# Two encoder layers: x stored by halves, a reordered beginning, and the second half's leading products between the layers taken from x without its token factors

## The chip, the cores and the metric

The kernel runs on one core of one Trainium2 chip. The metric is the device time of one execution in microseconds (us). The kernel before took 1564.54 us, the median of three runs (1564.0 to 1566.41). Its trace comes from one profiled execution. In the trace and in this text the engines are: PE or TensorE (products; PEld is its loading of weights), DVE or VectorE, ACT or ScalarE, POOL or GpSimd, and SP, whose queue issues most of the loads. ACTq and POOLq are the queues on which ScalarE and GpSimd issue loads.

## The reference

Two layers (DEPTH 2) of an encoder work on a residual stream x of 512 tokens by 1024 channels in float32. Cut to what matters:

```
mem_n = rms_norm(mem, mem_norm_g)
for l in range(DEPTH):
    h = rms_norm(x, g_pre_mix[l])
    proj = h @ w_in[l]
    q_a, k_a, v_a, q_b, k_b, v_b, q_m, gate_pre = split(proj)
    o_a = neighborhood_attention(q_a, k_a, v_a)      # 6 heads
    o_b = dilated_attention(q_b, k_b, v_b)           # 6 heads in 3 groups
    o_m = memory_attention(q_m, mem_n, w_mem_kv[l])  # 4 heads, 256 memory tokens
    merged = sum of sigmoid(gate_pre + b_gate) * (o @ w_br) over the three branches
    x = x + rms_norm(merged @ w_out[l], g_post_mix[l])
    h = rms_norm(x, g_pre_ffn[l])
    a, b = split(conv3(h @ w_up[l]))
    x = x + rms_norm((gelu(a) * b) @ w_down[l], g_post_ffn[l])
```

`rms_norm(x, g)` is `x * rsqrt(mean(x*x) + 1e-6) * g`, with the mean over the 1024 channels of a token. A token's factor, the reciprocal root, is one number per token; the gain g is one number per channel.

## The kernel before, in words

**Layout.** x is held transposed: channels on the 128 partitions in 8 chunks (KD = 8), 512 tokens along the free dimension. The tokens are worked in two halves of 256 (HALVES) wherever a norm has to be waited for. x lives in two tiles of four chunks by 512 tokens each; load_x fetches two chunks of one half in each of four DMAs (L190-L192).

**Products.** Each weight tile of 128 output channels is loaded raw in float32 on SP's queue (L225), and split into a high part by ScalarE and a low part (raw minus high) by VectorE or GpSimd (split, L218; weights, L222). Activations are split in the same way, and mm3 (L244) makes one product of three: high by high, high by low, low by high. In the trace all products of mm have line L242; transposes have L253; VectorE's and ScalarE's operations go through a counting wrapper and all have L114, so they are told apart by their tiles: whi and wlo (or m, h) from wraw are the split weights; h from x, vec, pt is a normed chunk; y, x, acc and sq belong to the ends of sublayers; ka are key tiles; pt, s, o and mm are banks of PSUM. There are three mm banks, two s banks, two pt banks and one o bank.

**Order of the work.** The class Woven writes TensorE's order by hand. It keeps a clock `clk` that adds a planned cost for each product, and a heap of jobs (Python generators) with due times: a job yields a delay or a flag to wait for, and is stepped when the clock has come to its due time, at the ticks between the products. So a job's small TensorE steps are placed among the large products by planned times (`yield 0.8`, `yield lat`). TensorE runs in that order; the order on the other engines is set by the framework's scheduler, which goes by the order of issue and by its own model of when an instruction is ready, and the buffers of one tag are handed out in turn.

**Small steps.** rstd_job (L321) makes the tokens' factors: products with a column of 1/1024 sum the squares over the partitions, ScalarE takes the root, VectorE the reciprocal, and a product with the identity spreads the factors over all partitions (L338). pre_norm_job (L359) then makes h by normed (L340): one VectorE operation with gain and factor, then a split. end_job (L373) ends a sublayer: it multiplies the sublayer's output by its factors, adds it to x, sums the squares of x and, if given, goes on with the next pre-norm. factor_end_job (L388) does the same but splits x times the gain without the token factors (raw_split); the factors R are multiplied in after the product. It serves the up-projection (after the mixing sublayer), not the boundary between the layers.

**The leading group.** The six projections that a layer begins with (FIRST: queries, keys and values of the first two head pairs) run as a group in pairs: run_group (L466) takes a pair of tiles through all eight chunks for one half of the tokens. Their banks come from group_banks (L463): two mm, two s, o and pt. The layer loop (L850) runs the group for the first half, then for the second; both wait for h of their half. Then a_q, a_k and a_v split the results, a_v also rearranges the values, and v_job transposes them. The first heads wait for the transposed values.

**The beginning.** The first half of x is loaded, squared and summed (first_squares, L825); then the first two weights are loaded and split, the second half of x is loaded, and the other four weights follow. vec, with all gains and biases, is loaded on GpSimd's queue near the top (L205).

**Between the layers.** In the down-projection of layer 0 (sublayer_end, L779) the last output tile is done by halves. At its beginning mem_norm_job is spawned for layer 1: it loads and norms the memory tokens, its squares by ScalarE and their sum by GpSimd (L316). The memory's key and value products of layer 1 (mem_kv) come after the last down-projection tile; mem_v_job transposes their values into an s bank. Then layer 1's leading group begins.

Of the kernel before, what the change touches and what calls it, by code (L numbers as in the profile page):

```python
# [14 lines left out]
SEQ = 512  # L15
# [12 lines left out]
FIRST = (0, 3, 6, 1, 4, 7)  # L28
# [91 lines left out]
def tile_hybrid_encoder(ctx, tc, xT, memT, memg, vecs, rpb, w_in, w_kv, w_bra, w_brb, w_brm,  # L120
# [84 lines left out]
    nc.gpsimd.dma_start(out=vec, in_=vecs)  # L205
# [115 lines left out]
    def rstd_job(accs, n, box):  # L321
# [37 lines left out]
    def pre_norm_job(l, goff, acc, hs, i):  # L359
        half, box = HALVES[i], []  # L360
        yield from rstd_job(acc if isinstance(acc, list) else [acc[:, half]], 256, box)
        for k in range(KD):
            normed(x[k][:, half], vec[:, l, goff + k:goff + k + 1], box[0], hs[k][0][:, half], hs[k][1][:, half],
                   G if k in LOG[l > 0 and goff == V_PRE] else V)
# [8 lines left out]
    def end_job(l, goff, og, acc, acc2, i, then, lat, more=()):  # L373
# [3 lines left out]
        for k in range(KD):  # L377
            V.tensor_mul(og[k][:, half], og[k][:, half], box[0])
            (G if then is None and i and k in TAILG else V).tensor_add(x[k][:, half], x[k][:, half], og[k][:, half])
            if acc2 is not None:  # L380
                sumsq_add(acc2[:, half], x[k][:, half], k == 0, None, G if k in SQG[goff == V_POSTF] else V)
            else:
                nc.sync.dma_start(out=out[:, k, half], in_=x[k][:, half])
# [4 lines left out]
    def factor_end_job(l, goff, og, acc, acc2, i, nxt):  # L388
# [5 lines left out]
        for k in range(KD):  # L394
            V.tensor_mul(og[k][:, half], og[k][:, half], box[0])
            V.tensor_add(x[k][:, half], x[k][:, half], og[k][:, half])
            raw_split(l, gnext, k, x[k][:, half], h[k][0][:, half], h[k][1][:, half])
# [4 lines left out]
        for k in range(KD):  # L402
            sumsq_add(acc2[:, half], x[k][:, half], k == 0)
# [4 lines left out]
        if i == 1:  # L408
            yield 0.6
            wv.give(f"R{l}.{gnext}")  # L410

# [51 lines left out]
    def group_banks():  # L463
        return [mmbank(), mmbank(), sbank(), sbank(), obank(128), tbank()]

    def run_group(grp, hs, half, flag, cols=None, side=2):  # L466
        if flag and side == 2:
# [3 lines left out]
        for i in range(0, len(ws), side):  # L471
            for k in range(n):
                if flag and side > 2:
                    wv.need(f"{flag}.{k}")
                rhs = [t[:, half] for t in hs[k]]
# [66 lines left out]
    def a_v(ps, qkv, flag):  # L542
# [5 lines left out]
        V.tensor_copy(vv[:, 0, :, 8:16], ps3[:, :, 0:8])  # L548
        V.tensor_copy(vv[:, 0, :, 0:8], ps3[:, :, 56:64])
# [229 lines left out]
    def sublayer_end(l, goff, w_of, rhs, n_half, then, lat=(1.4, 1.8), mid=None, fill=()):  # L779
# [26 lines left out]
        for i, half in enumerate(HALVES):  # L806
# [12 lines left out]
            if isinstance(then, tuple):  # L819
# [5 lines left out]
    def first_squares(half):  # L825
        sqs = [ytile((128, 256)) for _ in range(KD)]
        for k in range(KD):
            ACT.activation(sqs[k], x[k][:, half], AF.Square)
            if k % 2:
                V.tensor_add(sqs[k], sqs[k], sqs[k - 1])  # L830
            if k in (3, 5):
# [235 lines left out]
```

## Time and profile before

| | us |
|---|---|
| median of 3 runs | 1564.54 |
| profiled execution | 1565.1 |
| its span (first to last instruction) | 1563.3 |
| PE busy | 1524.4 |
| DVE busy | 945.2 |
| ACT busy | 735.1 |
| POOL busy | 155.2 |

A row of a timeline reads: start, time, engine, line, operation, out<-in, shape, how many were merged, and in brackets how long the engine had been idle and who ended that. Products are pipelined, so the time of a single one is longer than the distance to the next start; distances between starts are what the stream costs. A row of windows gives, for a stretch of time, each engine's busy time with its instructions, then the granted clock of TensorE (1.00 is full) and the DMA engines' share.

### The profile page before, as it was taken

The numbers are of one execution on the slowest core, as the hardware profiler recorded it, in microseconds if no ns is written. First come the engines' busy times: TensorE is split into PE (matmuls) and PEld (weight loads), VectorE is DVE, ScalarE is ACT, GpSimd is POOL, SyncE is SP. The second block draws the span as 40 slices with busy tenths as digits, with TensorE's granted clock in tenths as the row PEclk, the third lists the DMA queues.
The fourth block names the chain that finished last, engine by engine and source line by source line (L and its number), as shares of the span: only waits on it lengthen the run. The fifth ranks groups of instructions, "written<-read, shape, count | busy, mean of one in ns | idle before, by whom it ended". The sixth has DMA issues, their size and how long they took to land.

```text
span 1563.3 us, 20698 instructions
## 1 busy us (share of the span) xinstructions
PE 1524.4 (98%) x7994; PEld 1303.7 (83%) x7994; DVE 945.2 (60%) x1682; ACT 735.1 (47%) x1267; POOL 155.2 (10%) x219
## 2 busy tenths in 40 slices
PE   6999999999999999999989999999999999999997
PEld 6888888888988888788889888888889888888887
DVE  6685566235777777742385856753456877775233
ACT  5564575236544444522344645743364544444231
POOL 4340000210000000100061400001100000000000
PEclk9999999999999999999989999999999999999999
DMA  7222113325113322333331221132250222333331
GB/s 244 88 79 72 61 57 96 93 95 163 54 56 101 100 94 95 104 98 101 115 115 44 80 69 63 56 108 81 95 189 15 81 95 95 94 100 96 98 103 63
DMA packets 46610, 144.90 MB, mean 93 GB/s; under 512 B 5232, under 2 KB 11376, under 8 KB 46512
## 3 DMA queue, kind: packets, MB, share of 16 engines
q1 hardware_dynamic: 44656, 139.61, 28.2%
q10 hardware_dynamic: 1152, 2.10, 0.5%
q0 software_dynamic: 704, 1.88, 0.4%
q8 instruction: 62, 1.02, 0.3%
q14 instruction: 36, 0.29, 0.1%
HBM read 141.47 MB, written 2.10 MB: 92 GB/s over the span
## 4 chain that ended last, share of the span: by engine, by line
PE 54%; DVE 3%; issue 0%; ACT 0%; ACTq 0%; DVEq 0%
PE mm L242 48%; PE s L242 3%; PE o L242 2%; PE pt L242 1%; PE pt L253 1%; DVE y L114 1%; DVE x L114 1%; DVE m L114 0%; DVE acc L114 0%; DVE wlo L114 0%; DVE ka L114 0%; DVE st L114 0%; ACT sq L114 0%; ACT y L114 0%; ACT m L114 0%
## 5 line engine op out<-in xcount | busy, mean ns | idle before, releaser
L242 PE MATMUL mm<-h,whi 128*128 128x512 f32 x2496 | 775.7, 392 | 0.0
L242 PEld LDWEIGHTS mm<-h,whi 128*128 128x128 f32 x2496 | 461.5, 188 | 90.9
L242 PE MATMUL mm<-h,wlo 128*128 128x512 f32 x1248 | 486.4, 390 | 0.0
L114 DVE TENSOR_TENSOR wlo<-wraw,whi 128x1024 fp32r<-128x1024 f32 (+1 forms) x213 | 259.8, 1221 | 293.9 <-ACT whi L114 291.5
L114 ACT CAST whi<-wraw 128x1024 fp32r<-128x1024 f32 (+1 forms) x213 | 221.0, 1039 | 318.5 <-PE mm L242 310.4
L242 PEld LDWEIGHTS mm<-h,wlo 128*128 128x128 f32 x1248 | 234.3, 188 | 49.9
L242 PE MATMUL mm<-m,whi 128*128 128x512 f32 (+1 forms) x800 | 216.3, 358 | 2.7 <-ACT whi L114 1.8
L242 PEld LDWEIGHTS mm<-m,whi 128*128 128x128 f32 x800 | 142.5, 190 | 25.1 <-ACT whi L114 2.2
L242 PE MATMUL mm<-m,wlo 128*128 128x512 f32 (+1 forms) x400 | 142.8, 357 | 1.2 <-DVE wlo L114 1.2
L114 DVE SCALAR_TENSOR_TENSOR y<-y,vec,y 128x511 f32<-128x511 f32 x176 | 130.9, 750 | 3.5 <-ACT y L114 0.9
L114 DVE TENSOR_TENSOR y<-mm,R 128x512 f32<-128x512 f32 x82 | 56.4, 688 | 68.5 <-PE mm L242 68.5
L242 PEld LDWEIGHTS mm<-m,wlo 128*128 128x128 f32 x400 | 75.9, 190 | 12.5 <-DVE wlo L114 1.6
L766 POOL TENSOR_TENSOR m<-m,y 128x512 f32<-128x512 f32 x28 | 36.1, 1288 | 405.7 <-DVE y L114 405.7
L114 ACT ACTIVATE y<-y,vec 128x512 f32<-128x512 f32 x88 | 71.0, 813 | 2.2 <-DVE y L114 1.9
L242 PE MATMUL mm<-m,m 128*128 128x512 f32 x240 | 63.6, 395 | 0.0
L114 ACT ACTIVATE y<-y 128x512 f32<-128x512 f32 x44 | 27.8, 632 | 72.0 <-DVE y L114 71.5
L242 PE MATMUL s<-h,m 128*128 128x256 f32 x384 | 54.7, 290 | 5.4 <-DVE m L114 5.4
L114 ACT ACTIVATE y<-mm,vec 128x512 f32<-128x512 f32 (+1 forms) x91 | 57.4, 631 | 0.1
L242 PE MATMUL mm<-h,m 128*128 128x256 f32 x360 | 54.6, 298 | 2.8 <-DVE h L114 1.8
L114 ACT CAST m<-pt 128x512 fp32r<-128x512 f32 (+1 forms) x72 | 38.2, 539 | 40.4 <-PE pt L253 32.0
L114 DVE TENSOR_TENSOR acc<-acc,sq 128x256 f32<-128x256 f32 (+1 forms) x80 | 40.5, 507 | 26.2 <-ACT sq L114 24.6
L114 DVE TENSOR_TENSOR m<-pt,m 128x512 fp32r<-128x512 f32 (+1 forms) x72 | 45.0, 629 | 18.3 <-ACT m L114 17.4
(143 smaller groups left out, 1762.5 us busy)
## 6 DMA issues: line engine op xcount, KB each, us to landing
wraw<-in_w_in_dram SPq DMA_DIRECT2D x88, 512.0 KB, 3.4
wraw<-in_w_up_dram SPq DMA_DIRECT2D x88, 512.0 KB, 3.3
wraw<-in_w_down_dram SPq DMA_DIRECT2D x32, 512.0 KB, 3.5
wraw<-in_w_out_dram SPq DMA_DIRECT2D x16, 512.0 KB, 4.2
wraw<-in_w_down_dram SPq DMA_DIRECT2D x16, 384.0 KB, 3.1
wraw<-in_w_kv_dram SPq DMA_DIRECT2D x8, 512.0 KB, 4.4
wraw<-in_w_bra_dram SPq DMA_DIRECT2D x16, 192.0 KB, 2.3
x<-in_xT_dram SPq DMA_DIRECT2D x8, 256.0 KB, 6.9
```

The costliest lines, as they stand in the source:

```text
L114: return op(*args, **kw)
L242: wv.pe(nc.tensor.matmul(ps, a, b, start=first, stop=last), cost)
L253: wv.pe(nc.tensor.transpose(ps[:, 128 * i:128 * i + 128], s, ident), 0.11)
L766: (V if br == 2 and m >= 6 else G).tensor_add(acc[m], acc[m], gs)
```

## The change

- x is one tile of two halves, each of 8 chunks by 256 tokens, and the host lays xT out in the same way, so that a load of two chunks of a half is one run of 2 KB per partition. `xh(k, half)` replaces `x[k][:, half]` everywhere.
- The gains of layer 0's first norm come in a small tile g0 (128 by 8), loaded first on ScalarE's queue. vec moves from GpSimd's queue to SP's, behind the loads of the second half of x.
- first_squares adds the first half's squares only in pairs, and the sum over four tiles is left to the products.
- The low part of the second weight moves from GpSimd to VectorE. Two idle products of zeros into the o bank are put first in TensorE's order.
- The spread in rstd_job becomes a transpose.
- FIRST and group_banks change their order alike: each tile keeps its kind of bank, but the pair in o and pt comes second and the pair in the s banks last.
- Between the layers the second half goes through the new raw_end_job. Its leading products are taken from x times the gain, without token factors, as soon as each chunk is there; afterwards each of the six banks is multiplied by R for that half. h of the second half is also made, for the later projections.
- mem_norm_job of layer 1 is spawned with a delay of 20.
- The two edge copies in a_v move from VectorE to ScalarE.

```diff
-FIRST = (0, 3, 6, 1, 4, 7)
+FIRST = (0, 3, 4, 7, 6, 1)
...
-    xs = [const.tile([128, 4, 512], F32, name=f"x{i}") for i in range(2)]
-    x = [xs[k // 4][:, k % 4, :] for k in range(KD)]
+    xs = const.tile([128, 2, KD, 256], F32, name="x")
+
+    def xh(k, half):
+        return xs[:, half.start // 256, k, :]
...
-            nc.sync.dma_start(out=xs[k // 4][:, k % 4:k % 4 + 2, half], in_=xT[:, k:k + 2, half])
-
+            i = half.start // 256
+            nc.sync.dma_start(out=xs[:, i, k:k + 2, :], in_=xT[:, i, k:k + 2, :])
+
+    g0 = const.tile([128, KD], F32, name="g0")
+    nc.scalar.dma_start(out=g0, in_=vecs[:, 0, V_PRE:V_PRE + KD])
     load_x(HALVES[0])
...
-    nc.gpsimd.dma_start(out=vec, in_=vecs)
...
-            mm(pr[:, 128 * b:128 * b + 128], spread, ident, True, True, 0.22)
+            wv.pe(nc.tensor.transpose(pr[:, 128 * b:128 * b + 128], spread, ident), 0.11)
...
+    def raw_end_job(l, goff, og, acc, acc2, nxt, lat):
+
+
+        half, box = HALVES[1], []
+        hs, raw, R = nxt
+        yield lat
+        raw.extend((t[:, 0, :], t[:, 1, :]) for t in [ktile(F32R, (128, 2, 256)) for _ in range(KD)])
+        yield from rstd_job([acc[:, half]], 256, box)
+        for k in range(KD):
+            V.tensor_mul(og[k][:, half], og[k][:, half], box[0])
+            V.tensor_add(xh(k, half), xh(k, half), og[k][:, half])
+            raw_split(l + 1, V_PRE, k, xh(k, half), *raw[k])
+            if k == 0:
+                yield 0.6
+            wv.give(f"raw{k}")
+            yield 1.05
+        for k in range(KD):
+            sumsq_add(acc2[:, half], xh(k, half), k == 0)
+        yield 3.5
+        box = []
+        yield from rstd_job([acc2[:, half]], 256, box)
+        ACT.copy(R[:, half], box[0])
+        wv.give("R")
+        for k in range(KD):
+            normed(xh(k, half), vec[:, l + 1, V_PRE + k:V_PRE + k + 1], box[0], hs[k][0][:, half], hs[k][1][:, half])
+        crit[0] = last_copy[0]
+        yield 1.2
+        wv.give(f"h{l + 1}.{V_PRE}.1")
...
-        return [mmbank(), mmbank(), sbank(), sbank(), obank(128), tbank()]
+        return [mmbank(), mmbank(), obank(128), tbank(), sbank(), sbank()]
...
-        V.tensor_copy(vv[:, 0, :, 8:16], ps3[:, :, 0:8])
-        V.tensor_copy(vv[:, 0, :, 0:8], ps3[:, :, 56:64])
+        ACT.copy(vv[:, 0, :, 8:16], ps3[:, :, 0:8])
+        ACT.copy(vv[:, 0, :, 0:8], ps3[:, :, 56:64])
...
-            if k in (3, 5):
+            if k in (3, 5) and half != HALVES[0]:
                 V.tensor_add(sqs[k], sqs[k], sqs[k - 2])
-        return sqs[5::2]
-
+        return sqs[1::2] if half == HALVES[0] else sqs[5::2]
+
+    idle_bank = obank(128)
+
+    def idle(n):
+
+        one, none = mean[:, 0:1], zero[:, 0:1]
+        a, b = (bass.AP(t.tensor, t.offset, [list(t.ap[0]), [0, w]]) for t, w in ((one, 128), (none, 512)))
+        for _ in range(n):
+            mm(idle_bank, a, b, True, True, 0.0)
+
+    idle(2)
     hs = h_tiles()
     wv.spawn(pre_norm_job(0, V_PRE, first_squares(HALVES[0]), hs, 0))
-    gw = group_weights([w_in[0, m] for m in FIRST[:2]], (V, G))
+    gw = group_weights([w_in[0, m] for m in FIRST[:2]], (V, V))
     load_x(HALVES[1])
+    nc.sync.dma_start(out=vec, in_=vecs)
...
-        for i in range(2):
-            run_group((gw, pss), hs, HALVES[i], f"h{l}.{V_PRE}.{i}")
+        run_group((gw, pss), hs, HALVES[0], f"h{l}.{V_PRE}.0")
+        if l == 0:
+            run_group((gw, pss), hs, HALVES[1], f"h{l}.{V_PRE}.1")
+        else:
+            run_group((gw, pss), raw, FULL, "raw", HALVES[1], 2, True)
+            wv.need("R")
+            for ps in pss:
+                V.tensor_mul(ps[:, HALVES[1]], ps[:, HALVES[1]], R[:, HALVES[1]])
+            wv.need(f"h{l}.{V_PRE}.1")
...
-            wv.spawn(mem_norm_job(l + 1, hm, htile))
-            box, pre = [], []
+            wv.spawn(mem_norm_job(l + 1, hm, htile), 20.0)
+            pre, R, raw, box = [], rtile(), [], []
...
-            sublayer_end(l, V_POSTF, w_of, fs, 1, then, (1.4, LAT1), lambda: wv.spawn(kv_ahead()))
+            sublayer_end(l, V_POSTF, w_of, fs, 1, [then, (box, raw, R)], (1.4, LAT1), lambda: wv.spawn(kv_ahead()))
```

More of the change, by code (lines that the diff above doesn't have):

```diff
@@ L362, in pre_norm_job @@
         for k in range(KD):
-            normed(x[k][:, half], vec[:, l, goff + k:goff + k + 1], box[0], hs[k][0][:, half], hs[k][1][:, half],
+            g = g0[:, k:k + 1] if l == 0 and goff == V_PRE else vec[:, l, goff + k:goff + k + 1]
+            normed(xh(k, half), g, box[0], hs[k][0][:, half], hs[k][1][:, half],
                    G if k in LOG[l > 0 and goff == V_PRE] else V)
@@ L378, in end_job @@
             V.tensor_mul(og[k][:, half], og[k][:, half], box[0])
-            (G if then is None and i and k in TAILG else V).tensor_add(x[k][:, half], x[k][:, half], og[k][:, half])
+            (G if then is None and i and k in TAILG else V).tensor_add(xh(k, half), xh(k, half), og[k][:, half])
             if acc2 is not None:
-                sumsq_add(acc2[:, half], x[k][:, half], k == 0, None, G if k in SQG[goff == V_POSTF] else V)
+                sumsq_add(acc2[:, half], xh(k, half), k == 0, None, G if k in SQG[goff == V_POSTF] else V)
             else:
-                nc.sync.dma_start(out=out[:, k, half], in_=x[k][:, half])
+                nc.sync.dma_start(out=out[:, k, half], in_=xh(k, half))
         if then is not None:
@@ L395, in factor_end_job @@
             V.tensor_mul(og[k][:, half], og[k][:, half], box[0])
-            V.tensor_add(x[k][:, half], x[k][:, half], og[k][:, half])
-            raw_split(l, gnext, k, x[k][:, half], h[k][0][:, half], h[k][1][:, half])
+            V.tensor_add(xh(k, half), xh(k, half), og[k][:, half])
+            raw_split(l, gnext, k, xh(k, half), h[k][0][:, half], h[k][1][:, half])
             if k == 0:
@@ L410, in factor_end_job @@
             wv.give(f"R{l}.{gnext}")
+    def raw_end_job(l, goff, og, acc, acc2, nxt, lat):
[6 more added lines that the diff above has]
+            V.tensor_mul(og[k][:, half], og[k][:, half], box[0])
+            V.tensor_add(xh(k, half), xh(k, half), og[k][:, half])
+            raw_split(l + 1, V_PRE, k, xh(k, half), *raw[k])
[4 more added lines that the diff above has]
+        for k in range(KD):
+            sumsq_add(acc2[:, half], xh(k, half), k == 0)
+        yield 3.5
[8 more added lines that the diff above has]
+        wv.give(f"h{l + 1}.{V_PRE}.1")
     def h_tiles():
@@ L463, in group_banks, with run_group @@
     def group_banks():
-        return [mmbank(), mmbank(), sbank(), sbank(), obank(128), tbank()]
-    def run_group(grp, hs, half, flag, cols=None, side=2):
-        if flag and side == 2:
+        return [mmbank(), mmbank(), obank(128), tbank(), sbank(), sbank()]
+    def run_group(grp, hs, half, flag, cols=None, side=2, each=False):
+        each = each or side > 2
+        if flag and not each:
             wv.need(flag)
@@ L472, in run_group @@
             for k in range(n):
-                if flag and side > 2:
-                    wv.need(f"{flag}.{k}")
-                rhs = [t[:, half] for t in hs[k]]
+                if flag and each:
+                    wv.need(f"{flag}{k}")
+                rhs = [t[:, half] if half != FULL else t for t in hs[k]]
                 for w, ps in zip(ws[i:i + side], pss[i:i + side]):
@@ L818, in sublayer_end @@
                         post_norm_tile(l, goff, m, ps, og, acc, half, n0 == 0 and len(order) + len(pair) == KD and m == pair[0])
-            if isinstance(then, tuple):
+            if isinstance(then, list) and i:
+                wv.spawn(raw_end_job(l, goff, og, acc, acc2, then[1], lat[1]))
+            elif isinstance(then, list):
+                wv.spawn(end_job(l, goff, og, acc, acc2, 0, lambda i: then[0](acc2, i), lat[0]))
+            elif isinstance(then, tuple):
                 wv.spawn(factor_end_job(l, goff, og, acc, acc2, i, then))
@@ L900, in tile_hybrid_encoder @@
         for i in range(2):
-            run_group((gw, list(pss.values())), hs, HALVES[i], f"h{l}.{V_PREF}.{i}", None, 4)
+            run_group((gw, list(pss.values())), hs, HALVES[i], f"h{l}.{V_PREF}.{i}.", None, 4)
         fs, held, flag = [], [], f"R{l}.{V_PREF}"
```

10 lines of the change are left out of this document (4 added, 6 removed).

## The prediction

> **What bounds the kernel now.** I read the page first, then TensorE's timeline over the whole span for every wait it shows, then the timelines of the other engines around the three longest waits.
>
> ```profile
> span 1563.3 us, 20698 instructions
> PE 1524.4 (98%) x7994; PEld 1303.7 (83%) x7994; DVE 945.2 (60%) x1682; ACT 735.1 (47%) x1267; POOL 155.2 (10%) x219
> ```
>
> The profiled execution took 1565.1 us, 1.8 us more than its span; the median of the runs shown is 1564.54, or 0.6 us below it. TensorE is busy for 98% of the span. So an edit pays only where TensorE stands still, where its clock drops after it stood still, or where its own work shrinks. The products stay the same in number. The first place is the start:
>
> ```profile
> 9.04 1.84 PE L242 MATMUL pt<-mean,y 128*128 128x1 f32 x8 [9.04 <-DVE y L114]
> ...
> 11.43 1.22 PE L242 MATMUL pt<-ident,st 128*128 128x128 f32 x4 [0.55 <-DVE st L114]
> ...
> 16.08 7.33 PE L242 MATMUL mm<-h,m 128*128 128x256 f32 x41 [1.84 <-DVE h L114]
> ```
>
> The second is the entry into the down-projection of layer 0. TensorE waits for a high part and then for a low part of the weights:
>
> ```profile
> 660.60 0.61 PE L242 MATMUL mm<-m,whi 128*128 128x512 f32 x2
> 661.06 0.39 PE L242 MATMUL mm<-m,wlo 128*128 128x512 f32 x1
> 663.26 0.74 PE L242 MATMUL mm<-m,whi 128*128 128x512 f32 x2 [1.81 <-ACT whi L114]
> 665.20 0.50 PE L242 MATMUL mm<-m,wlo 128*128 128x512 f32 x1 [1.20 <-DVE wlo L114]
> ...
> 669.87 0.62 PE L242 MATMUL mm<-m,whi 128*128 128x512 f32 x2
> ```
>
> The third is the boundary between the layers:
>
> ```profile
> 779.08 0.60 PE L242 MATMUL pt<-ident,st 128*128 128x128 f32 x4
> 779.44 0.48 PE L242 MATMUL mm<-m,whi 128*128 128x256 f32 x2
> ...
> 791.52 0.58 PE L242 MATMUL pt<-mean,acc 128*128 128x1 f32 x4 [1.43 <-DVE acc L114]
> ...
> 801.43 0.50 PE L242 MATMUL pt<-mean,acc 128*128 128x1 f32 x4
> ...
> 807.01 0.52 PE L242 MATMUL s<-h,m 128*128 128x256 f32 x3
> 812.91 7.13 PE L242 MATMUL s<-h,m 128*128 128x256 f32 x45 [5.37 <-DVE m L114]
> 819.88 0.52 PE L242 MATMUL o<-h,m 128*128 128x256 f32 x3
> ...
> 826.51 5.92 PE L242 MATMUL mm<-h,m 128*128 128x256 f32 x48
> 832.27 5.92 PE L242 MATMUL s<-h,m 128*128 128x256 f32 x48
> ```
>
> From the last two rows one pair of tiles takes 5.76 us for one half of the tokens (832.27 − 826.51), 0.12 us a product. The 45 products from 812.91 to 819.88 took 6.97 us where 45 × 0.12 = 5.4 are due; the missing 1.57 us are clock, as the granted clock shows:
>
> ```profile
> 790.00:800.00 10.00, 8.57 (x60) 8.51 (x60) 7.56 (x21) 5.18 (x15) 7.71 (x21) 0.83 0.31 102
> 810.00:820.00 10.00, 7.09 (x46) 7.12 (x47) 6.96 (x17) 2.98 (x8) 4.83 (x6) 0.68 0.33 112
> ```
>
> (columns: PE, PEld, DVE, ACT, POOL, granted clock, DMA share, GB/s).
>
> **The change part by part.**
>
> *Boundary, order of the banks.* TensorE does three products of the second pair at 807.01 and then waits 5.37 us. The two tiles of that pair lie in the two s banks, and the one it waits for still holds memory values of the next layer; they are read out here:
>
> ```profile
> 812.35 0.41 DVE L114 TENSOR_TENSOR m<-s,m 128x256 fp32r<-128x256 f32 x1
> ```
>
> The new order puts the pair of the o and pt banks second and the s banks third. That gives the read-out one pair more, 5.76 us: the s bank is wanted at 807.01 + 5.76 = 812.8 and comes free at about 812.8. Five pair-halves were left at 807.01, so with two small steps of 0.36 us (779.08 to 779.44) the group would end at 807.01 + 28.8 + 0.7 = 836.5. In the trace it ends at 843.79, a row that comes below. So 7.3 us can be had.
>
> *Boundary, second half without factors.* What is late next? The second half's h would be; its statistics are complete only after VectorE's stretch:
>
> ```profile
> 803.60:817.30 13.70, 8.33 (x57) 8.15 (x57) 13.34 (x26) 5.86 (x14) 7.07 (x7) 0.75 0.50 163
> ```
> ```profile
> L114 DVE SCALAR_TENSOR_TENSOR h<-x,vec,pt x32: 467/472/487, 12.7 to 828.6; 128x256 f32<-128x256 f32 x32
> ```
>
> VectorE was busy 13.34 of 13.70 us there. Products from raw x need no statistics, so TensorE goes on at 807.01 + 11.5 + 0.4 = 818.9. The price: eight low parts on VectorE (nearest row 0.47 us, 3.8 us in all) and eight high parts on ScalarE, which was busy only 5.86 us of that stretch, and then six multiplications of the banks by R. The last four of those lie under the remaining products, those of the last pair cost at most about 0.5 us each behind the group and hide behind the projection that has its own bank. But the chain to the second half's sum of squares gets longer: it ended at 817.3 and would end at about 821. Its TensorE step is placed by the issue order: 801.43 plus the delays in the new job (0.8 + 0.6 + 8 × 1.05 + 3.5 = 13.3 us on the planner's clock, each rounded up to the next step of six products, 0.64 us on that clock, some 16.6 in all; the planner counts 0.107 a product where the trace has 0.12, so 18.7 real), at about 820. So a wait of 0 to 4 us, taken as 1.3, and 0 to 1.5 for the s bank, taken as 1. Boundary: 7.3 − 2.3 = **5.0 us** gained, bounds 0 and 7.3. The eight raw tiles take ka buffers, of which there are twelve; the keys of the first head pair take the other four, those of the second wait until the last pair's products end, and are wanted later than that. The wait at 791.52 is left as it is: nothing in its chain changes.
>
> A wait of a microsecond is not free here: after the 1.43 us at 791.52 the granted clock over 790 to 800 is 0.83, so 10 × 0.17 = 1.7 us were lost for it. [...]
>
> *Small steps once.* Every root-mean-square step spreads its two columns by transposes instead of fp32 products. There are 72 records of the old form, four to a step, so 18 steps:
>
> ```profile
> L242 PE MATMUL pt<-ident,st x72: 270/275/582, 11.4 to 1555.1; 128*128 128x128 f32 x72
> ```
> ```profile
> 843.79 0.63 PE L242 MATMUL mm<-h,whi 128*128 128x512 f32 x2
> ...
> 851.31 0.60 PE L253 MATMUL pt<-ident,sq 128*128 128x128 f32 x4
> ...
> 862.65 0.60 PE L253 MATMUL pt<-ident,y 128*128 128x128 f32 x4
> 863.00 0.71 PE L242 MATMUL mm<-h,whi 128*128 128x512 f32 x2
> ```
>
> Four transposes take 0.35 us of the stream (862.65 to 863.00), two 0.18, against 0.36 for the old step. I count 16 steps inside the stream: 16 × 0.18 = **2.9 us**, bounds 2 and 3.3; the two of the start are in the start's chain. [...] The rows show half, and the sum goes by the rows.
>
> *Memory norm 20 us later.* At the entry of the down-projection ScalarE stands behind its squares, which wait for GpSimd:
>
> ```profile
> 658.28 7.45 POOL L316 TENSOR_TENSOR h<-h,sq 128x256 f32<-128x256 f32 x7 [301.60 <-ACT sq L114]
> ...
> 662.17 1.77 ACT L114 CAST whi<-wraw 128x1024 fp32r<-128x1024 f32 x2
> ```
>
> GpSimd takes 7.45 us for seven additions, the squares wait for its buffers, and the weights' cast comes at 662.17, after TensorE has run dry at about 661.3. From 661.06 to 669.87 there are 16 products, due 16 × 0.23 = 3.7 us (660.60 to 661.06 is two) and taking 8.81, so 5.1 us are lost, waits and clock. Moved by 20 us, the four memory loads on ScalarE's queue, the squares and the additions meet ScalarE with one cast per eight k steps and no convolution. I take **4.5 us**, bounds 0 (the same block in front of another cast) and 5.1. The normed memory is first used far behind, at the boundary, so it is not late.
>
> *The start.* Its chain is: last x landing, square, sum, mean, root, spread, h.
>
> ```profile
> 3.51 1.42 ACT L114 ACTIVATE y<-x 128x256 f32<-128x256 f32 x4 [1.26 <-DMA x<-in_xT_dram]
> ...
> 11.72 0.69 DVE L114 TENSOR_TENSOR m<-wraw,m 128x512 fp32r<-128x512 f32 x1 [0.34 <-ACT m L114]
> ...
> 12.81 2.94 POOL L220 TENSOR_TENSOR m<-wraw,m 128x512 fp32r<-128x512 f32 x2 [6.03 <-ACT m L114]
> 13.09 1.53 DVE L114 TENSOR_TENSOR m<-wraw,m 128x512 fp32r<-128x512 f32 x1
> ```
>
> The loads of x now move whole rows of two chunks, and vec's load goes behind the second half on SP's queue; in its way there stand only the third weights and later. I give the last landing 0 to 0.9 us, taken as 0.4. Two additions fewer on VectorE and the spread by transposes (1.22 us for four cold records, half of that for two) give 0.6. The second weights' low part leaves GpSimd: VectorE pays two more splits of 0.69, but its own split no longer takes 1.53 beside GpSimd, and TensorE no longer waits for 12.81 + 2.94 = 15.75; together about 1.5. g0's load goes onto ScalarE's queue ahead of the first square, which waited 1.26 us for x anyway; without that cover it would cost its issue, under half a microsecond. The two idle products run before the first 9 us are over, when TensorE has nothing to do; TensorE is then empty again for microseconds, and by the clock of 0.83 after 1.43 us I give them nothing. Start: 0.4 + 0.6 + 1.5 = **2.5 us**, bounds 0 and 4.5. The values' edge copies on ScalarE instead of VectorE and the first group's order in layer 0 I take as nothing; they lie under products.
>
> **Sum.** 5.0 + 2.9 + 4.5 + 2.5 = 14.9 us; 1565.1 − 14.9 = 1550.2 for a profiled execution, 0.6 less for a median: **1549.6 us**. About 0.2% (3 us) is what a measurement of this kernel can tell from no change.
>
> **The rivals.** *A, the boundary's gain turns into a new wait.* For: VectorE is full there and gets 3.8 us more. Against: ScalarE and TensorE have room, and no raw product needs the sum. If TensorE waits for the second half's sum of squares as long as it did for the s bank, boundary 0: 1554.6 us. *B, the memory norm's block moves with it.* For: the squares are still paced by GpSimd, and a cast of weights comes every five microseconds. Against: layer 1's entry, without a memory norm, shows no wait in TensorE's timeline. Gain 0 there: 1554.1; A and B together 1559.1. *C, slower: the first heads start late.* In both layers the values of the first head pair (tile 6) now end with the last pair, and their banks are multiplied by R first in layer 1; if their transposes stand in TensorE's order before the copies are done, TensorE stops behind them. Each late microsecond costs one per layer, two over both; to eat the 14.9 us they must be 7.5 us late in each. At 10 us each: 1549.6 + 20 = 1569.6. Against: the old transposes stood 7.5 us behind the group's end (851.31 against 843.79), which leaves room for a multiplication and three copies. *D, nothing of it shows*, because the scheduler moves as much elsewhere: 1564.
>
> **How the numbers follow.** Forecast 0.60, A 0.13, B 0.12, A and B 0.04, C 0.07, D 0.04. At their upper bounds (7.3, 5.1, 4.5 and 3.3) the terms give 20.2 us, so 1544.3, and a wait at 791.52 that shrinks by the way can add one: 1543. Upward the forecast reaches to 1554, where A and B begin, and with them the range is **1543 to 1559**; C and D are outside. Faster by over 0.2% is the forecast, A, B and both, less a little for mixtures: 0.86; within 0.2% 0.06; slower 0.08.
>
> **What would show it.** Right: the first stream of products starts near 13.5 us; no wait of over a microsecond near 661 us; no 5.37 us wait in the s bank; the leading group ends about 13 us earlier than 843.79 on the span's clock (start, entry, boundary and the small steps so far); x36 records of transposes where x72 products stood. Wrong: a wait for VectorE's acc inside the raw products (A), a late cast near 681 us (B), a wait for sq at the first heads (C).

## The result, and the profile after

The changed kernel takes 1555.05 us (median of 4 executions, 1552.91 to 1556.01) against 1564.89 us for the kernel before in the same comparison: a ratio of 0.9934, 95% interval 0.9917 to 0.9951. A second set of five executions gave 1553.9 us, ratio 0.9923 (0.991 to 0.9936). So it is faster, by 10 to 12 us, and the predicted 1549.6 us is some 5 us too low. The profiled execution took 1552.91 us, span 1550.9 us, and was the fastest of its four; against the profiled execution before it gained 12.2 us.

The head of the page of the changed kernel, span and busy time of each engine:

```profile
span 1550.9 us, 20677 instructions
PE 1522.6 (98%) x7970; PEld 1300.1 (84%) x7970; DVE 948.8 (61%) x1684; ACT 739.7 (48%) x1288; POOL 148.6 (10%) x216
```

TensorE's timeline of the changed kernel follows, at the places that the prediction showed of before (start, length, line, operation, count, and the idle time ahead with what ended it):

```profile
13.28 7.23 PE L246 MATMUL mm<-h,m 128*128 128x256 f32 x41 [0.91 <-DVE h L114]
21.90 1.05 PE L246 MATMUL pt<-mean,y 128*128 128x1 f32 x8 [1.40 <-DVE y L114]
...
652.92 0.62 PE L246 MATMUL mm<-m,whi 128*128 128x512 f32 x2
653.37 0.39 PE L246 MATMUL mm<-m,wlo 128*128 128x512 f32 x1
...
784.97 0.64 PE L246 MATMUL pt<-mean,acc 128*128 128x1 f32 x4 [3.44 <-DVE acc L114]
...
799.87 0.52 PE L246 MATMUL o<-h,m 128*128 128x256 f32 x3
...
805.63 5.92 PE L246 MATMUL s<-h,m 128*128 128x256 f32 x48
811.39 2.29 PE L246 MATMUL mm<-ka,m 128*128 128x256 f32 x18
814.83 0.58 PE L246 MATMUL pt<-mean,acc 128*128 128x1 f32 x4 [1.16 <-DVE acc L114]
...
830.42 0.62 PE L246 MATMUL mm<-h,whi 128*128 128x512 f32 x2
...
840.75 0.65 PE L257 MATMUL pt<-ident,sq 128*128 128x128 f32 x4 [0.86 <-ACT sq L114]
...
874.37 0.55 PE L257 MATMUL pt<-ident,y 128*128 128x128 f32 x3 [2.11 <-DVE y L114]
```

The reader should see five things. The first stream starts at 13.28 instead of 16.08, but a new wait of 1.40 us stands at 21.90. The entry into the down-projection (652.92) has no wait. The wait for acc at the boundary has grown from 1.43 to 3.44 us. The s banks come third and nobody waits for them; the products from raw x (operand ka) start at 811.39, and the wait for the statistics behind them is 1.16 us. And at 874.37, in the heads of layer 1, stands a wait of 2.11 us that the kernel before did not have. The leading group ends at 830.42, 13.4 us before the 843.79 of before.

The spreads by transposes, as one group of the changed kernel:

```profile
L341 PE MATMUL pt<-ident,st 128*128 128x128 f32 x36 | 7.8, 300 | 1.1 <-DVE st L114 1.1
```

That is half the records of before (x72). What one step costs the stream shows in the distance to the next start, 0.14 us in the changed kernel and 0.36 before:

```profile
416.45 0.38 PE L341 MATMUL pt<-ident,st 128*128 128x128 f32 x2
416.59 0.97 PE L246 MATMUL s<-h,m 128*128 128x256 f32 x6
```

```profile
418.70 0.60 PE L242 MATMUL pt<-ident,st 128*128 128x128 f32 x4
419.06 0.96 PE L242 MATMUL s<-h,m 128*128 128x256 f32 x6
```

Now the gain of the profiled execution, stage by stage, from the starts of the same instruction in both timelines:

| stretch on TensorE | before | after | gained, us | predicted |
|---|---|---|---|---|
| start, to the first memory product of layer 0 | 63.25 | 61.56 | 1.7 | 2.5 |
| from there to the step at 250.23 / 248.07 | 186.98 | 186.51 | 0.5 | 0 and part of the small steps |
| entry of the down-projection, 655.84 / 652.92 to 671.92 / 663.80 | 16.08 | 10.88 | 5.2 | 4.5 |
| boundary, 784.17 / 775.61 to 843.79 / 830.42 | 59.62 | 54.81 | 4.8 | 5.0 |
| heads of layer 1, to 949.12 / 937.91 | 105.33 | 107.49 | -2.2 | 0 |
| small steps elsewhere (250 to 655, rest of the down-projection, 949 to the last spread) | | | 0.8 + 0.4 + 1.3 = 2.5 | 2.9, with those of the boundary |

The start's row is that of one execution. The ten other profiles of kernels with the changed start and the spreads by transposes (one without the idle products) have their first memory product between 60.09 and 61.89 us, so that the gain against 63.25 lies between 1.4 and 3.2 us.

Together 12.5 us at the last spread (1554.66 against 1542.14), of which 12.4 are left in the span.

### The profile page after: what moved, and what is told of

The parts are those of the page before. It is cut to its first block, busy times and chain, and to the rows that moved or that the text cites. A ratio compares the mean times of both kernels' runs of the same rounds, so it can differ in the third digit from the quotient of the medians.

```text
span 1550.9 us, 20677 instructions
## 1 busy us (share of the span) xinstructions
PE 1522.6 (98%) x7970; PEld 1300.1 (84%) x7970; DVE 948.8 (61%) x1684; ACT 739.7 (48%) x1288; POOL 148.6 (10%) x216
## 4 chain that ended last, share of the span: by engine, by line
PE 91%; DVE 5%; ACT 2%; DMA 1%; issue 1%; SPq 0%; ACTq 0%; DVEq 0%
PE mm L246 80%; PE s L246 4%; PE o L246 3%; PE pt L257 2%; DVE y L114 1%; DVE m L114 1%; PE pt L246 1%; DVE x L114 1%; DVE ka L114 1%; DVE acc L114 1%; ACT y L114 0%; DMA vec<-in_vecs_dram 0%; DVE wlo L114 0%; ACT m L114 0%; ACT whi L114 0%
## 5 line engine op out<-in xcount | busy, mean ns | idle before, releaser
L114 ACT ACTIVATE y<-y,st 128x256 f32<-128x256 f32 (+1 forms) x80 | 43.7, 547 | 26.7 <-DVE st L114 26.6
L114 ACT CAST m<-y 128x512 fp32r<-128x512 f32 x32 | 19.8, 619 | 72.5 <-DVE y L114 72.5
```

Source lines behind the costliest of these rows:

```text
L114: return op(*args, **kw)
```

## The experiments

Each edit is made on the changed kernel unless it is said otherwise, and is compared with its 1553.9 and 1555.05 us. A ratio is always to the kernel before in the same comparison. That kernel's median was 1564.13 to 1566.22 us in these comparisons, so a difference of two medians from different ones is uncertain by about 2 us. A dip of the clock means that the granted clock falls to 0.5 for a few microseconds, as from 785 to 789 us in the changed kernel: 0.67, 0.50, 0.50 and 0.62 by single microseconds, 1.7 us lost.

**No products from raw x.** The second half's leading products wait for the normed h again, in the new order of banks.

```diff
-        if l == 0:
-            run_group((gw, pss), hs, HALVES[1], f"h{l}.{V_PRE}.1")
-        else:
-            run_group((gw, pss), raw, FULL, "raw", HALVES[1], 2, True)
...
+        run_group((gw, pss), hs, HALVES[1], f"h{l}.{V_PRE}.1")
```

The second half goes through end_job and pre_norm_job again.

> The changed kernel with the second half between the layers taken the old way (end job, then h with its factors), all else as changed. Theory: the raw job is worth about 3 us where it stands, because without it the second half's leading products wait for h (VectorE is full until about 815 us), but it costs about 2 us ahead of that: its tiles hold the ka buffers, so GpSimd's small casts into the key tiles no longer stand between its weight splits, the splits follow one another and block VectorE, and the wait for acc before the first pre-norm grew from 1.43 to 3.44 us. So here that wait is 1 to 2 us again, a wait of 2 to 4 us appears at the second half's first product, and the time is 1554 to 1558 us. Rival: the wait before the pre-norm has nothing to do with the raw job (bank order or the later memory norm made it); then it stays above 3 us here and the time is 1557 to 1560.

Measured: 1552.15 us (1549.8 to 1554.17), ratio to before 0.9923 (0.9909 to 0.9938). That is below the expected 1554 to 1558 us: the largest piece of code in the change brings nothing that can be measured. TensorE's timeline without it:

```profile
781.87 0.58 PE L246 MATMUL pt<-mean,acc 128*128 128x1 f32 x4 [1.55 <-DVE acc L114]
807.18 0.58 PE L246 MATMUL pt<-mean,acc 128*128 128x1 f32 x4 [2.35 <-DVE acc L114]
814.48 3.74 PE L246 MATMUL mm<-h,m 128*128 128x256 f32 x29 [0.30 <-DVE h L114]
```

The second half waits 2.35 + 0.30 us here instead of 1.16, so the raw products do hide 1.5 us. But the wait for acc is 1.55 us instead of 3.44, and no wait stands in the heads of layer 1. What the raw products give at one place they take at two others. The wait at acc is that of the first theory, 1 to 2 us.

**The old order of tiles and banks.**

```diff
-FIRST = (0, 3, 4, 7, 6, 1)
+FIRST = (0, 3, 6, 1, 4, 7)
...
-        return [mmbank(), mmbank(), obank(128), tbank(), sbank(), sbank()]
+        return [mmbank(), mmbank(), sbank(), sbank(), obank(128), tbank()]
```

> The changed kernel with the old order of the leading group (the pair in the s banks second, the pair in o and pt last), all else as changed. Theory: the wait in the s bank comes back; the memory values are read out at about 805.3 us, the bank is wanted at about 800, so 4 to 6 us wait and 1 to 2 us of clock: 1560 to 1562 us. Rival: the raw job alone has taken the 5.37 us away, since the group no longer needs the second half's h; then no such wait and at most 1 us slower, 1555 to 1556.

Measured: 1559.88 us (1559.3 to 1562.25), ratio 0.9975 (0.9966 to 0.9984), 5 to 6 us worse than the change by the medians and 6 to 8 by the ratios. The old wait is back:

```profile
805.91 4.39 PE L246 MATMUL s<-h,m 128*128 128x256 f32 x19 [5.39 <-DVE m L114]
```

So the boundary's gain comes from the order, not from the raw products.

**Memory norm without the 20 us.**

```diff
-            wv.spawn(mem_norm_job(l + 1, hm, htile), 20.0)
+            wv.spawn(mem_norm_job(l + 1, hm, htile))
```

> The changed kernel with the memory norm spawned without the delay, all else as changed. Theory: the squares go ahead of the weights' cast on ScalarE again at the entry of the down-projection, TensorE waits there for whi and wlo about 3 us and runs 2 us of slow clock: 4 to 5.5 us slower, 1559 to 1561. Rival: the other edits have shifted the scheduler so that the cast comes first anyway; then no wait at the entry and the same time, 1554 to 1556.

Measured: 1559.68 us (1558.19 to 1563.55), ratio 0.9973 (0.9964 to 0.9983), 5 to 6 us worse by the medians and 6 to 8 by the ratios. Both waits are back, 3.0 us together, and 3.4 us of clock go behind them:

```profile
659.40 0.73 PE L246 MATMUL mm<-m,whi 128*128 128x512 f32 x2 [1.82 <-ACT whi L114]
661.33 0.79 PE L246 MATMUL mm<-m,wlo 128*128 128x512 f32 x1 [1.20 <-DVE wlo L114]
```

**Spreads by products again.**

```diff
-            wv.pe(nc.tensor.transpose(pr[:, 128 * b:128 * b + 128], spread, ident), 0.11)
+            mm(pr[:, 128 * b:128 * b + 128], spread, ident, True, True, 0.22)
```

> The changed kernel with the spread of the token factors done by fp32 products again, all else as changed. Theory: 16 steps of 0.18 us in the stream and some tenths in the start's chain: 2.5 to 3.5 us slower, about 1558. [...] Rival two: it hides, because most steps fall beside waits of TensorE; then under 1 us.

Measured: 1565.32 us (1559.84 to 1567.35), ratio 1.0003 (0.9992 to 1.0013): 10 to 11 us worse by the medians, not 2.9. In the profiles the last spread stands 1554.75 − 1542.14 = 12.6 us later. From 937.91 (here 949.29) to that spread TensorE needs 1.2 us more, and that fits the term. The rest is in other rows of its timeline and granted clock:

```profile
788.74 0.58 PE L246 MATMUL pt<-mean,acc 128*128 128x1 f32 x4 [4.31 <-DVE acc L114]
820.83 0.98 PE L246 MATMUL pt<-mean,acc 128*128 128x1 f32 x4 [3.52 <-DVE acc L114]
```

```profile
820.00:825.00 5.00, 4.17 (x19) 4.20 (x20) 0.75 (x3) 0.26 (x1) 0.00 (x0) 0.51 0.00 0
825.00:830.00 5.00, 5.00 (x37) 5.00 (x36) 4.12 (x12) 2.76 (x7) 0.00 (x0) 0.81 0.01 3
```

(columns as in the prediction: PE, PEld, DVE, ACT, POOL, granted clock, DMA share, GB/s). The wait for the statistics is 3.52 us instead of 1.16, and 5 × 0.49 + 5 × 0.19 = 3.4 us of clock go behind it, where the changed kernel lost none. With 0.9 us more at acc and a further dip of 1.7 us near 887, that is 2.4 + 3.4 + 0.9 + 1.7 = 8.4 us beside the steps. Another 1.7 us stand at the start, where the first memory product comes at 63.23 instead of 61.56. Part of this is chance: the profile of the changed kernel that is used here has fewer dips than the other one (below). Why the statistics come that much later was not separated; the planner's price of the step also goes from 0.11 to 0.22 and shifts the issue order.

**Casts between the splits.** The first theory for the grown wait at acc: in the kernel before GpSimd's zero casts into the ka tiles stood between its weight splits, and VectorE's additions got on beside them (two took 0.75 us at 783.74, against 1.98 beside a split at 780.39); in the change the raw tiles hold ka buffers, and the casts come 29 us later (812.48 instead of 783.48). GpSimd of the kernel before:

```profile
778.05 5.48 POOL L220 TENSOR_TENSOR m<-wraw,m 128x512 fp32r<-128x512 f32 x4 [112.32 <-ACT m L114]
783.48 0.38 POOL L536 CAST ka<-zero 128x8 fp32r<-128x8 f32 x1
...
784.15 1.49 POOL L220 TENSOR_TENSOR m<-wraw,m 128x512 fp32r<-128x512 f32 x1
```

The edit puts casts on GpSimd ahead of two splits again.

```diff
                     yield GWD
+                    for _ in range(10):
+                        G.tensor_copy(pause, zero)
```

> The changed kernel, with ten 8-column casts on GpSimd ahead of each of the two weight splits that it does during the last products of w_down; the raw products stay. Theory: the wait for acc grew from 1.43 to 3.44 us because the casts into ka that stood between GpSimd's splits in the kernel before now come 30 us later, and the splits follow one another and hold up VectorE's additions of two tiles (2.2, 1.85 and 1.82 us for two, against 0.74 where GpSimd casts). Then the wait comes back to 1.4 to 2.4 us and the time falls by 1 to 3 us, to 1552 to 1554. Rival: the chain of the norm is late because the products ahead of it end 2.6 us sooner for VectorE (transposes, shorter steps), whatever GpSimd does: the wait stays at 3.2 to 3.6 us and the time within 1 us of the changed kernel's.

Measured: 1553.74 us (1553.41 to 1556.18), the wait at acc 3.45 us. It tells nothing about the theory: the casts depend on nothing but a constant, and all 20 ran at 6.0 to 11.4 us, at the start of the kernel. So it is one more run of the changed kernel.

**The first two w_in splits on VectorE.** This takes GpSimd out of the last microseconds ahead of acc.

```diff
-SQG, LOG, GEN, KVE = {0: (), 1: ()}, {0: (), 1: ()}, 'GGVGVG', 'VVGG'
+SQG, LOG, GEN, KVE = {0: (), 1: ()}, {0: (), 1: ()}, 'VVVGVG', 'VVGG'
```

> The changed kernel, with the first two of the next layer's w_in splits on VectorE instead of GpSimd. [...] Rival (VectorE's own amount of work is what counts): the wait grows to 4 us or more, the time to 1556 to 1559.

Measured: 1548.79 us (1547.08 to 1550.42), ratio 0.9893 (0.988 to 0.9905): 5 to 6 us faster than the change, the lowest median of all, and far below the 1556 to 1559 us that were expected if VectorE's own amount of work is what counts. GpSimd and then VectorE of the changed kernel:

```profile
769.69 6.92 POOL L224 TENSOR_TENSOR m<-wraw,m 128x512 fp32r<-128x512 f32 x5 [105.58 <-ACT m L114]
778.00 4.24 POOL L224 TENSOR_TENSOR m<-wraw,m 128x512 fp32r<-128x512 f32 x3 [1.39 <-ACT m L114]
```

```profile
771.81 2.21 DVE L114 TENSOR_TENSOR x<-x,y 128x256 f32<-128x256 f32 x2
773.94 0.74 DVE L114 TENSOR_TENSOR y<-y,pt 128x256 f32<-128x256 f32 x2
...
775.38 1.85 DVE L114 TENSOR_TENSOR x<-x,y 128x256 f32<-128x256 f32 x2
...
781.03 1.82 DVE L114 TENSOR_TENSOR x<-x,y 128x256 f32<-128x256 f32 x2
```

And VectorE of this experiment, where GpSimd is done at 773.9, with TensorE's step:

```profile
770.48 2.21 DVE L114 TENSOR_TENSOR x<-x,y 128x256 f32<-128x256 f32 x2
...
774.06 0.75 DVE L114 TENSOR_TENSOR x<-x,y 128x256 f32<-128x256 f32 x2
...
778.07 0.75 DVE L114 TENSOR_TENSOR x<-x,y 128x256 f32<-128x256 f32 x2
778.74 0.68 DVE L114 TENSOR_TENSOR m<-wraw,m 128x512 fp32r<-128x512 f32 x1
...
780.28 0.41 DVE L114 TENSOR_TENSOR acc<-acc,sq 128x256 f32<-128x256 f32 x1
780.63 0.69 DVE L114 TENSOR_TENSOR m<-wraw,m 128x512 fp32r<-128x512 f32 x1
```

```profile
780.84 0.58 PE L246 MATMUL pt<-mean,acc 128*128 128x1 f32 x4 [0.64 <-DVE acc L114]
```

Two additions of two SBUF tiles take 0.75 us when GpSimd is quiet and 1.8 to 2.2 us beside its splits, each of which is 1.4 us long: the pair loses 1.1 to 1.5 us. Two multiplications with one operand in PSUM (y<-y,pt) take 0.74 us beside the same splits. Why the additions lose time there and the multiplications do not, no run shows. VectorE took four more splits of 0.68 us, two of them ahead of the sum at 780.28 that TensorE's step waited for and two behind it. Counted from the end of w_down, the acc step still came 2.8 us sooner (780.84 − 774.28 against 784.97 − 775.61).

**All four on VectorE.** The last two w_kv splits as well ('VVVV' for KVE).

```diff
-SQG, LOG, GEN, KVE = {0: (), 1: ()}, {0: (), 1: ()}, 'GGVGVG', 'VVGG'
+SQG, LOG, GEN, KVE = {0: (), 1: ()}, {0: (), 1: ()}, 'VVVGVG', 'VVVV'
```

> The changed kernel with the first two w_in splits and also the last two w_kv splits of the next layer on VectorE, so that GpSimd does nothing beside the norm's additions between 768 and 781 us. [...] If VectorE's own work is the limit now (it runs without a gap from 769.8 us on in the run with the w_in splits there), the four further subtractions of 0.68 us cost 2.7 us against 1.5 saved: a wait for acc of 1.5 to 2.5 us, and 1549 to 1551.5 us.

Measured: 1553.14 us (1551.01 to 1554.4), ratio 0.9921 (0.9907 to 0.9934), slower than the expected 1549 to 1551.5 us. The two additions at 771 take 0.76 us, where two took 2.21 in the run before, and nobody waits for acc at the step that stood at 780.84. But the statistics of the second half are now late:

```profile
771.32 0.76 DVE L114 TENSOR_TENSOR x<-x,y 128x256 f32<-128x256 f32 x2
```

```profile
792.25 0.40 PE L341 MATMUL pt<-ident,st 128*128 128x128 f32 x2 [0.88 <-DVE st L114]
...
812.49 0.98 PE L246 MATMUL pt<-mean,acc 128*128 128x1 f32 x4 [3.11 <-DVE acc L114]
```

That wait was 1.08 us in the run before, and 3.4 us of clock go behind it. VectorE's later additions stand beside GpSimd's next splits (two take 2.20 us at 793.36). Whether that or VectorE's greater load makes the wait was not separated.

**Both: no raw products, and the w_in splits on VectorE.** The edits are those of the two runs above.

```diff
-            run_group((gw, pss), raw, FULL, "raw", HALVES[1], 2, True)
...
+        run_group((gw, pss), hs, HALVES[1], f"h{l}.{V_PRE}.1")
...
-SQG, LOG, GEN, KVE = {0: (), 1: ()}, {0: (), 1: ()}, 'GGVGVG', 'VVGG'
+SQG, LOG, GEN, KVE = {0: (), 1: ()}, {0: (), 1: ()}, 'VVVGVG', 'VVGG'
```

> The changed kernel without the raw products, and with the first two w_in splits of the next layer on VectorE. If the two losses are separate: the wait for acc falls to 0.6 us as in the run with the splits alone (1548.8 us), the wait at the heads near 869 (1.85 us, with a dip of the clock worth 1.7 us) goes, and the second half's first product waits 2.3 to 2.7 us for its norm instead of 1.1: 1546 to 1548 us. Rival: the raw products only cost where VectorE is held up, and with the splits moved they pay: then this one is slower than 1548.8, at 1550 or more.

Measured: 1550.12 us (1549.44 to 1551.53), ratio 0.9906 (0.9891 to 0.9921). With raw products it was 0.9893 (0.988 to 0.9905): the two cannot be told apart. The trace has 0.72 us at acc, no wait in the heads, and 2.26 us for the second half's statistics with a dip of the clock. So with those splits moved, too, no run shows that the raw products pay: what they save at the boundary they cost again in the heads, within what can be measured.

**The start alone**, on the kernel before: x by halves, g0, both first splits on VectorE, the shorter sum of squares, the idle products.

```diff
+    g0 = const.tile([128, KD], F32, name="g0")
+    nc.scalar.dma_start(out=g0, in_=vecs[:, 0, V_PRE:V_PRE + KD])
...
+    idle(2)
...
-    gw = group_weights([w_in[0, m] for m in FIRST[:2]], (V, G))
+    gw = group_weights([w_in[0, m] for m in FIRST[:2]], (V, V))
     load_x(HALVES[1])
+    nc.sync.dma_start(out=vec, in_=vecs)
```

> The kernel before with the start of the changed one alone (x by halves, the short first copy of the norm's factors, both first splits on VectorE, two idle products); boundary, order, small steps and memory norm as before. The prediction's term is 2.5 us, so 1561.6 us. The rival is that the first stream starts 2.5 to 2.8 us sooner and loses part of it at the norm of the second half near 22 us, so that 0.5 to 1.7 us are left: 1562.5 to 1563.7.

Measured: 1564.43 us (1560.04 to 1569.19), ratio 0.999 (0.9978 to 1.0002). That is 3.4 us of gain to 0.3 of loss, so it can be told neither from none nor from the 2.5 predicted. Its profiled execution shows where a part is lost:

```profile
14.65 6.88 PE L247 MATMUL mm<-h,m 128*128 128x256 f32 x41 [0.91 <-DVE h L114]
23.09 0.61 PE L247 MATMUL pt<-mean,y 128*128 128x1 f32 x4 [1.56 <-DVE y L114]
24.49 0.60 PE L247 MATMUL pt<-mean,y 128*128 128x1 f32 x4 [0.80 <-DVE y L114]
64.15 0.47 PE L247 MATMUL mm<-m,whi 128*128 128x256 f32 x2 [0.85 <-DVE m L114]
```

The stream starts 1.4 us sooner than before and then waits 2.4 us for the second half's squares, which VectorE finishes no sooner. In the kernel before this step stood at 23.50 with no wait at all. Behind the waits 1.7 us of clock go here, and the first memory product comes at 64.15 (63.25 before). The run is not the prediction's term undone as a whole, since that counts the spread by transposes in. The run with the spreads by products stands at 63.23 there, and every profile with transposes at 60.09 to 61.89.

**No idle products.**

```diff
-    idle(2)
```

> The changed kernel without the two idle products at the start. The prediction gave them nothing: a median of 1553 to 1556 us, as the changed kernel's 1553.9 to 1555.1. [...]

Measured: 1556.55 us (1554.89 to 1559.97), ratio 0.995 (0.9935 to 0.9966). The median is 1.5 to 2.7 us above the change's, and the intervals overlap. In its profile the first memory product stands at 61.37 and the acc step at 784.86, as in the changed kernel (61.56 and 784.97). Whether they are worth something stays open; that they cost something is not seen. Of the nine profiles with idle products taken by then, five show the granted clock fall to 0.5 between 10 and 15 us (no raw products, old order, no delay, spreads by products, start alone). In the first three of these it was at 0.5 from 10 to 15 us, and the first memory product still came at 60.09 to 60.55, no later than in the changed kernel.

**The v copies back on VectorE.**

```diff
-        ACT.copy(vv[:, 0, :, 8:16], ps3[:, :, 0:8])
-        ACT.copy(vv[:, 0, :, 0:8], ps3[:, :, 56:64])
+        V.tensor_copy(vv[:, 0, :, 8:16], ps3[:, :, 0:8])
+        V.tensor_copy(vv[:, 0, :, 0:8], ps3[:, :, 56:64])
```

> The changed kernel with the two short copies of the v evacuation back on VectorE. The prediction gave them nothing: within 1 us of the changed kernel. Rival: they are on the path of the wait at the v transposes (0.86 us behind ScalarE's sq; 1.10 behind VectorE's in the kernel before), so that putting them back costs the 0.25 us of that and a longer queue on VectorE: 0.5 to 2 us more.

Measured: 1553.11 us (1552.67 to 1554.36), ratio 0.9925 (0.991 to 0.994): no difference. The waits at the v transposes grow from 0.80 to 1.31 and from 0.86 to 1.10 us, and the one in the heads shrinks from 2.11 to 1.42; 0.75 against 0.69 us.

**The changed kernel again.**

> The changed kernel once more, to bring its interval down: its first four executions lay between 1552.9 and 1556.0 us, and its profiled one was the fastest of them. Both theories expect a median of 1554 to 1556 us; a median under 1553 would mean that the run without the raw products (1552.15 us) is no faster.

Measured: 1553.9 us (1551.99 to 1556.28). Its profiled execution was the slowest of its five, the other one the fastest of its four, and so the pair shows what differs between two executions of one kernel. First the granted clock of the first set's profile, then of this one:

```profile
785.00:790.00 5.00, 5.00 (x30) 5.00 (x31) 3.72 (x11) 2.30 (x7) 3.07 (x8) 0.66 0.02 7
```

```profile
785.00:790.00 5.00, 4.75 (x22) 4.78 (x23) 3.37 (x10) 2.45 (x8) 3.08 (x8) 0.52 0.07 25
790.00:795.00 5.00, 5.00 (x37) 5.00 (x36) 3.42 (x11) 2.21 (x7) 0.00 (x0) 0.80 0.00 0
...
875.00:880.00 5.00, 3.92 (x16) 3.27 (x17) 2.96 (x5) 2.63 (x4) 3.21 (x6) 0.74 0.00 0
880.00:885.00 5.00, 5.00 (x32) 4.50 (x31) 3.89 (x11) 1.90 (x6) 2.17 (x3) 0.92 0.37 131
```

Behind the same wait (3.44 and 3.46 us) one lost 5 × 0.34 = 1.7 us of clock and the other 5 × 0.48 + 5 × 0.20 = 3.4. Behind the wait in the heads (2.11 and 2.09 us) one lost nothing and the other 5 × 0.26 + 5 × 0.08 = 1.7. That is 3.4 us, and the spans differ by 1554.3 − 1550.9 = 3.4.

## Why the prediction was right, and where it was wrong

**Direction and mechanism held.** The order of banks, the memory norm's delay and the spreads each carry about what they were given or more, and the rivals A (the gain turns into a wait for the statistics: 1.16 us, predicted 1.3) and B (the norm's block moves with it: no wait at the entry) did not come. The sign that the prediction named for A, a wait for acc inside the raw products, is there, at the size that it had put into the sum: the step was to stand 18.7 us behind 801.43, and TensorE reached it 18.3 us behind the same step (795.36 to 813.67). Of the 14.9 us the profiled execution gained 12.5: the heads took 2.2, the start gave 0.8 less and the entry 0.7 more. The medians lie further off, at 4.3 and 5.5 us above 1549.6, since that execution was the fastest of its four; the other profiled one lost 3.4 us more of clock.

**The boundary's 4.8 us for 5.0 are luck in part.** The wait at acc took 2.0 us that the prediction did not have, and two things gave them back: the microsecond for the s bank did not come, and an estimated 0.7 us of cheaper small steps (three at 0.23, below) are in the 4.8.

**"The wait at 791.52 is left as it is: nothing in its chain changes" failed.** Apart from the shorter spread no instruction of the chain was touched, but what stood beside it was: GpSimd's zero casts moved away, its splits closed up, and VectorE's additions beside them took 1.8 to 2.2 us for two. The wait grew by 2.0 us. The run with those splits on VectorE has 0.64 us and is 5 to 6 us faster, more than the 2.8 us of the wait, since the dip of the clock behind it goes too (TensorE's granted clock is 1.00 from 780 to 800 us there). That GpSimd's splits make the wait is shown. That it was the raw tiles' hold on the ka buffers that let them close up has one run for it: without raw products the casts stand between the splits again (773.90 to 782.48), and the wait is 1.55 us. VectorE does the same eight multiplications, eight additions and seven sums ahead of the step in both runs, in 13.83 us (771.14 to 784.97) against 11.94 (769.93 to 781.87). The run that was to add casts alone did not place them.

**The raw products were priced at one place only.** Behind the acc wait the boundary gained 6.8 us, which is the 7.3 less the 1.16 of the new wait and plus the 0.7 of three cheaper steps; without the order 5 to 6 us of the change's gain are gone, without the raw products none. The prediction gave VectorE's 3.8 us more of low parts a price only at the second half's sum. Every kernel with raw products has a wait of 1.4 to 2.4 us in the heads of layer 1, and the two without them have none there. It is not the wait that rival C named: the values' transposes wait 0.86 us for sq, where they waited 1.10 before. TensorE stands a step later, before the transposes of the heads' y. The rows of VectorE ahead of 874.37 show only that it is late for the last y; which part of the raw job makes it late was not separated.

**The start was counted to the first stream only.** What is late next was not asked. The stream did start 2.8 us sooner. The 0.4 us for the last landing was the author's estimate, and no run takes it alone: in the two profiled executions ScalarE ended the last square of the first half at 6.43 + 1.44 = 7.87 us, where it had been 8.31 + 0.72 = 9.03. The issue of g0's load took 0.41 us on ScalarE's queue. But the second half's statistics follow eight microseconds later on a VectorE that is full (busy 8.45 of the 8.62 us from 13.28 to 21.90), and they came only 23.50 − 21.90 = 1.6 us sooner. Up to the memory products 1.7 us are left in the profiled execution, with 1.7 us of clock lost behind the new wait. Over the profiles it is 1.4 to 3.2, so the size of 2.5 is not refuted; that the start's edits gain it without the transposes is not shown.

**The small steps were priced too low, and undoing them costs more than their sum.** The prediction measured four transposes of a head (0.35 us) and took half, 0.18 us saved a step. Eleven steps outside the start and the boundary saved 2.5 us, 0.23 each, since two spreads take 0.14 us of the stream and not 0.18. For 16 steps that is an estimate of 3.7 us, above the 2.9 and their bound of 3.3. Undone, they cost 10 to 11 us. Two of them stand in the chains for which TensorE waits at the boundary, those waits are 0.9 and 2.4 us longer there, and clock is lost behind them; how much of the longer waits the steps themselves make was not separated.

**The entry: right amount, wrong picture.** 5.2 us were gained for 4.5. But the block did not move by 20 us. ScalarE and GpSimd of the changed kernel:

```profile
654.57 1.03 ACT L114 CAST whi<-wraw 128x1024 fp32r<-128x1024 f32 x1
```

```profile
656.30 7.81 POOL L320 TENSOR_TENSOR h<-h,sq 128x256 f32<-128x256 f32 x7 [301.78 <-ACT sq L114]
```

GpSimd's additions stand at 656.30, where they stood at 658.28; counted from the entry they moved 0.9 us (3.4 us behind 652.92, 2.4 behind 655.84). The delay only let the weights' cast go ahead of the squares (654.57 instead of 662.17), and that was enough.

**The clock.** The prediction read 1.7 us of clock for a short wait from the row of 0.83, though no term of its sum is named for it. Behind 1.43 us in the kernel before and behind 1.40 us (at 21.90) in the changed one stands a dip of 1.7 us each (792 to 796 and 24 to 28 us). But the rows speak against a fixed price: 2.09 us cost 1.7 us of clock in one execution of the changed kernel, and 2.11 at the same place nothing in the other.

## What to carry to other kernels

An engine's chain can get slower although none of its instructions is touched: where VectorE adds two SBUF tiles on the path, look at what GpSimd does in those microseconds (here two such additions took 0.75 us, or 1.8 to 2.2 beside its splits), and at what kept GpSimd from doing it until now. When a stretch is brought forward, follow it to the next point where TensorE needs another engine, and price the new work at every such point, not only at the one that the change aims at. Undo each part alone: here the smallest edits (an order of six numbers, a delay, a transpose, the letters of two splits) carry the time, and the longest one nothing that can be measured. A time up to a point in one profile holds for one execution: look at the same point in the other runs before calling a term wrong.

## What the runs showed of the hardware

The loss of clock came in steps. Between 20 us and the last products it was 1.7 or 3.4 us behind each wait that had one, that is one dip or two, 3.4 or 6.8 us at half speed. Behind single pauses of up to 1.31 us none was seen (1.08 us with the w_in splits on VectorE, 1.16 in the changed kernel, 1.28 at 79.26 in the kernel before, 1.31 with the v copies back on VectorE), behind pauses of 1.4 to 2.4 us none (2.11 in the changed kernel) or one (1.43 in the kernel before, 2.26 in the run with both), behind those over 3 us one (3.44 in the changed kernel's first profile) or two (5.37 in the kernel before, 3.11 with all four splits on VectorE). The two waits at the entry of the down-projection, 1.8 and 1.2 us close together, cost none (the start alone), one (the kernel before) or two (no delay). So a wait of two microseconds cost two (2.11 us) or nearly four (2.09 and 1.7 of clock), and the traces do not show what decides it. In the one pair of executions of one kernel that was compared, the spans differ by two whole dips, 3.4 us.
